# A two-layer encoder trunk on one core: new costs in the planner that writes the instruction order

## The chip, the cores and the metric

The kernel runs on 1 core of one Trainium2 chip. The metric is the device time of one execution in microseconds (us); lower is better. The time of a kernel is the median of its runs.

## The reference, cut to what matters

The input is 2048 frames of 1024 channels in float32, with one conditioning vector c. There are two layers; each computes `x = x + gate * Mixer(RMSNorm(x) * (1 + scale) + shift)`, where shift, scale and gate are linear functions of SiLU(c). A last RMSNorm follows.

```python
# layer 0, RG-LRU
proj = h @ in_w                      # 1024 -> 2 * 1024
xb = causal_dwconv(xb, conv_w) + conv_b            # width 4
gates = sigmoid(einsum('bsni,knij->kbsnj', xg, gate_w) + gate_b)   # 8 blocks of 128, two gates
a_t = exp(-8 * r_t * softplus(-lam));  b_t = sqrt(1 - a_t**2) * i_t * xf
h_t = a_t * h_(t-1) + b_t;  out = (h * silu(zg)) @ out_w
# layer 1, gated DeltaNet, 8 heads of 128, chunks of 64
q, k, v = silu(causal_dwconv(h @ in_w))            # q and k normalised
t_mat = inverse of the unit lower triangle of each chunk
v_new = u_c - w_c @ state;  o_c = q_c @ state + attn_c @ v_new      # chunk after chunk
state = state * e_c + k_c.T @ v_new
out = (rmsnorm(o) * silu(z)) @ out_w
```

## The kernel before

**Work and stages.** Everything large is a product on TensorE (PE). Operands are split into a high and a low part (hi, lo), and each product is hi*hi + hi*lo + lo*hi: 24 matmuls of 128x512 for one panel of 128 output channels and one half of 512 tokens (`products`, matmul on L653). These "panel products" are called mm in the profile (mmo for the output projections). There are 6168 of them. Tokens come in two units of 1024 (u = 0, 1), each with two halves (i = 0, 1). The stages follow one another: conditioning and norm, `in1` of unit 0 and 1 (layer 0), `out1`, `in2` of unit 0 and 1 (layer 1), `out2`. All the rest of a layer is done beside its panel products, on the engines that are free, and with small matmuls that stand between the panel products on PE.

**Layer 0 beside `in1`.** For every block n of 128 channels and every half i: the product of panel x is copied to `xe` (ACT, L713); the convolution is a first tap on GpSimd (POOL, `xf`, L727) and three taps on VectorE (DVE, `xf`, `taps`, L701); `gates_thread` casts the result to `xh` (ACT, L751), subtracts to `xl` (DVE, L754), and multiplies both with the gate weights, three matmuls for each of two gates (PE, `pg`, L760, PSUM buffers of the tag "c", two of them). ACT makes tanh (L810), tanh and exp (L770, L772) and a square root (L783), DVE a scan (L791), POOL the last product `tz` (L798), which goes to memory. The square root is in another table of ACT than the rest, so ACT loads a table before it and after it (ACT_TABLE_LOAD). The panel's hi part is a cast on ACT (`whi`, L639), the lo part a subtraction on POOL (`wlo`, 128x1024, L642). The other conditioning rows are sums on DVE (`acc`, L415).

**Layer 1 beside `in2`.** For every head h: the convolutions as above (taps again L701), products of keys (PE, `pk` L1073, `pkk` L1108, `pqk` L1193), inverses of the 32 x 32 triangles on DVE in 31 pairs of steps (`ttmp` L1228, `tblk` L1231), the larger blocks on PE (`px`, `pr`, "levels"), and then the recurrence, 16 chunks of 128 tokens, of which each is a chain through three engines (`recurrence_thread`): `pp` = k.state, q.state on PE (L1348, L1349), `zt` on DVE (L1357), `py` on PE (L1365), `yt` on ACT (L1371), `pS` on PE (L1377, L1378), `state` on DVE (L1390), and again. Reciprocal square roots of norms are a power on POOL, of 128x4 elements (L249).

**What sets the order.** Nothing is written by hand in order. A planner, class `Weave`, runs when the kernel is built. Each piece of work is a thread (a Python generator) that, before it emits an instruction, yields the engine, an estimated duration in us, and optionally the latency until the thread's next step can start. `Weave.run` always takes the thread whose step can start earliest by these estimates and lets it emit its instruction:

```python
return max(th.t, self.free.get(w[0], 0.0))        # start of a step: thread and engine free
...
self.free[w[0]] = t + w[1]
th.t = t + w[1] + (w[2] if len(w) > 2 else self.LAG[w[0]])
```

On the chip every engine then takes its instructions in that order, one after the other, and waits by semaphores for what they need; an instruction that waits holds up all that stands behind it on its engine. The estimates are in no instruction. They decide only which instruction stands before which, on each of the five queues (PE, ACT, DVE, POOL, and SP, which issues the DMAs). The panel products have the lowest priority and fill what is free on PE.

Of the kernel before, what the change touches and what calls it, by code (L numbers as in the profile page):

```python
# [36 lines left out]
class Event:  # L37
    t = None
# [3 lines left out]
class Slots:  # L42
    """The buffers of a tag, taken in turn."""
# [5 lines left out]
class Hold:  # L49
    """A buffer with several last readers."""  # L50
# [15 lines left out]
class Weave:  # L66
    """Emits threads of instructions in the order of their estimated start.

    Before each step a thread yields the engine, its duration and optionally the latency
    until the next step may start; for a transfer "sp", its bytes and whether to wait for  # L70
    its end. It yields an Event to wait for it, and Slots to take a buffer of them.
    """

    SEEN = 0.92
    LAG = {"pe": 0.2, "act": 0.3, "dve": 0.3, "pool": 0.2}

    def __init__(self):
        self.free = dict.fromkeys(("pe", "act", "dve", "pool", "sp", "dma"), 0.0)
        self.threads = []
        self.now = 0.0  # L80
# [19 lines left out]
    def start(self, th):  # L100
# [8 lines left out]
        return max(th.t, self.free.get(w[0], 0.0))  # L109

    def run(self):
        while self.threads:
# [17 lines left out]
            elif w[0] == "none":  # L130
                th.t = t + max(w[1], 0.0)
            else:
                self.free[w[0]] = t + w[1]
                th.t = t + w[1] + (w[2] if len(w) > 2 else self.LAG[w[0]])
# [4 lines left out]
def trunk_kernel(ctx, tc, x, c, ada_w, ada_b, ada_c, norm_c, final_g, w1, cw1, cb1, gate_w, gate_b, lam, ow1,  # L139
# [24 lines left out]
    # constants  # L164
# [37 lines left out]
    # tags: pool and number of buffers  # L202
# [11 lines left out]
    # free after the queries, before the recurrence ends  # L214
# [29 lines left out]
    STT, EV, CP, TR, MM, M4 = 0.665, 0.605, 0.48, 0.109, 0.2163, 0.218  # L244
# [6 lines left out]
    def softplus(out, src, e, d):  # L251
        # max(x, 0) + log1p(exp(-|x|)), log1p(e) = 2 atanh(e / (2 + e))
# [16 lines left out]
    def finish_columns(layer, part, d, src):  # L269
        # bias, and for the scale (1 + scale) * norm_g  # L270
# [9 lines left out]
    def columns_of(acc, pt):  # L280
        # sums over the partitions, four columns of 128 channels
# [5 lines left out]
    def first_loads_thread():  # L287
        # scale and shift of the first layer, in the order in which they are needed
# [35 lines left out]
    def first_pe_thread():  # L324
        # scale, by the tensor engine
        c_bc, ttok = yield ev("cbc")
        for n in (0, 2):
# [8 lines left out]
            yield "dve", 0.61, 0.13  # L336
# [4 lines left out]
            yield "dve", 0.61, 0.13  # L341
# [6 lines left out]
    def first_dve_thread():  # L348
        # shift, by DVE and the ones
# [47 lines left out]
    def row_halves_thread(parts):  # L397
        # halves of the other conditioning rows, summed over the channels of c by DVE and the ones
        row = tile_([P, D], "g1", "gate0")
        yield ev("gw", 0, 2)  # L400
        for layer, part, d in parts:
# [35 lines left out]
            yield "dve", 0.61  # L437
# [34 lines left out]
    def norm_thread(key, layer, src, t0, slot, before, after, xtags=("b4",) * TB, htag="hf"):  # L472
        # before: what the loads wait for; after: what the writes wait for
# [1248 lines left out]
```

## Time and profile before

| what | value |
|---|---|
| median of 3 runs | 2044.7 us (2042.34 to 2049.82) |
| profiled execution, first to last instruction (span) | 2033.7 us |
| PE busy | 1881.4 us (93%), 10408 matmul records |
| PE weight loads busy | 1526.0 us (75%) |
| DVE busy | 1578.4 us (78%) |
| ACT busy | 1019.8 us (50%) |
| POOL busy | 945.0 us (46%) |
| granted TensorE clock, mean | 0.978 |
| DMA | 263.99 MB, 130 GB/s |

The page gives the span of the profiled execution and no other time of it; the median of the runs is 11.0 us above that span, for what lies before the first and after the last instruction. The busy time of an engine counts from an instruction's start to its end, with what it loses in between: an instruction of DVE that is held up after its start counts as busy. A fp32 matmul of 128x128 is two records. Lines (L653) are lines of the kernel before; the changed kernel's lines are 15 higher below the planner.

### The profile page before, as it was taken

To read this page: it belongs to the slowest core of one execution; us is meant where nothing else is said; L and a number is where in the kernel's file an instruction comes from. 1 tells how busy PE (TensorE), PEld (TensorE's weight loads), DVE (VectorE), ACT (ScalarE), POOL (GpSimd) and SP (SyncE) were. 2 spreads that over 40 slices of the span, in tenths; PEclk is the share of its full clock that TensorE was granted. 3 is DMA by queue.
4 is the path that set the end of the run, shared out by engine and by line. 5 is a ranking of instruction groups with operands and counts; after the bars stand their busy time and mean duration, and the time that the engine had idled before them with its cause. 6 is when DMAs were issued, how large, how long until landed. Compare 5 with 4: busy or idle time off the path is not lost.

```text
span 2033.7 us, 31640 instructions
## 1 busy us (share of the span) xinstructions
PE 1881.4 (93%) x10408; PEld 1526.0 (75%) x10408; DVE 1578.4 (78%) x3176; ACT 1019.8 (50%) x2449; POOL 945.0 (46%) x1487
## 2 busy tenths in 40 slices
PE   6989889888999999999999999998999999999998
PEld 3777667676787777777787787777878777778887
DVE  6788998987744556988887988778888879887654
ACT  3656566454611224456565555554655555655311
POOL 4565665645400137545454653474455546531101
PEclk9999989989999999999999999999999999999999
DMA  8254524333368813436663436343334333466761
GB/s 315 60 150 128 186 98 134 122 109 119 125 195 215 252 54 96 102 70 148 143 144 82 89 86 173 84 113 93 69 91 104 90 79 83 111 184 210 227 197 63
DMA packets 493132, 263.99 MB, mean 130 GB/s; under 512 B 369188, under 2 KB 437028, under 8 KB 492968
## 3 DMA queue, kind: packets, MB, share of 16 engines
q1 hardware_dynamic: 492968, 261.97, 46.7%
q8 instruction: 82, 1.34, 0.3%
q14 instruction: 82, 0.67, 0.1%
HBM read 186.38 MB, written 75.50 MB: 129 GB/s over the span
## 4 chain that ended last, share of the span: by engine, by line
PE 39%; DVE 27%; DMA 8%; POOL 7%; issue 7%; ACT 6%; SPq 3%; DVEq 0%; POOLq 0%; ACTq 0%
PE mm L653 16%; PE mmo L653 12%; DVE xf L701 7%; DVE tblk L1231 3%; DVE ttmp L1228 3%; PE pg L760 2%; DMA raw<-in_w 2%; POOL wlo L642 1%; DVE ec L1100 1%; DMA xt_d<-xb 1%; SPq L515 1%; DVE acc L415 1%; POOL tz L798 1%; POOL xf L727 1%; DMA xt<-x_d 1%
## 5 line engine op out<-in xcount | busy, mean ns | idle before, releaser
L701 DVE SCALAR_TENSOR_TENSOR xf<-xe,cw_s,xf 128x512 f32<-128x512 f32 x384 | 359.8, 940 | 47.7 <-POOL xf L727 24.6
L642 POOL TENSOR_TENSOR wlo<-raw,whi 128x1024 fp32r<-128x1024 f32 x96 | 243.5, 2537 | 134.9 <-ACT whi L639 119.1
L1231 DVE TENSOR_TENSOR tblk<-tblk,ttmp 128x60 f32<-128x60 f32 (+24 forms) x496 | 144.3, 291 | 10.9 <-POOL tblk L1222 0.5
L1228 DVE TENSOR_TENSOR ttmp<-blk,tblk 128x60 f32<-128x60 f32 (+24 forms) x496 | 123.0, 248 | 16.9 <-DMA blk<-blk_d 6.5
L639 ACT CAST whi<-raw 128x1024 fp32r<-128x1024 f32 x96 | 100.2, 1044 | 47.3 <-DMA raw<-in_w 42.9
L716 POOL COPY carry<-xe 128x4 f32<-128x4 f32 x128 | 41.3, 322 | 170.6 <-ACT xe L713 158.8
L713 ACT COPY xe<-mm 128x512 f32<-128x512 f32 x128 | 74.1, 579 | 83.8 <-PE mm L653 79.8
L653 PE MATMUL mmo<-oh,yh 128*128 128x512 f32 x256 | 100.9, 394 | 5.1 <-DVE xr L908 4.7
L653 PE MATMUL mm<-hl_('in2', 1)_12407,whi 128*128 128x512 f32 x256 | 104.8, 410 | 0.0
L653 PE MATMUL mm<-hh_('in2', 0)_5394,whi 128*128 128x512 f32 x256 | 104.7, 409 | 0.0
L653 PE MATMUL mm<-hh_('in2', 0)_5171,whi 128*128 128x512 f32 x256 | 104.3, 407 | 0.3 <-ACT xe L713 0.3
L653 PE MATMUL mm<-hl_('in2', 0)_5395,whi 128*128 128x512 f32 x256 | 104.2, 407 | 0.0
L653 PE MATMUL mm<-hl_('in2', 1)_12235,whi 128*128 128x512 f32 x256 | 104.2, 407 | 0.0
L653 PE MATMUL mm<-hh_('in2', 0)_5394,wlo 128*128 128x512 f32 x256 | 104.1, 407 | 0.0
L653 PE MATMUL mm<-hh_('in2', 1)_12406,whi 128*128 128x512 f32 x256 | 104.0, 406 | 0.0
L653 PE MATMUL mm<-hl_('in2', 0)_5172,whi 128*128 128x512 f32 x256 | 103.8, 406 | 0.0
L653 PE MATMUL mm<-hh_('in2', 0)_5171,wlo 128*128 128x512 f32 x256 | 103.8, 405 | 0.0
L653 PE MATMUL mm<-hh_('in2', 1)_12234,whi 128*128 128x512 f32 x256 | 103.4, 404 | 0.2 <-DVE tz L972 0.2
L653 PE MATMUL mm<-hh_('in2', 1)_12406,wlo 128*128 128x512 f32 x256 | 103.6, 405 | 0.0
L653 PE MATMUL mm<-hh_('in2', 1)_12234,wlo 128*128 128x512 f32 x256 | 103.5, 404 | 0.0
L653 PE MATMUL mmo<-ol,oh 128*128 128x512 f32 (+1 forms) x264 | 102.1, 387 | 0.0
L653 PE MATMUL mmo<-oh,yl 128*128 128x512 f32 x256 | 100.8, 394 | 1.4 <-DVE yl L882 1.4
(326 smaller groups left out, 5910.8 us busy)
## 6 DMA issues: line engine op xcount, KB each, us to landing
raw<-in_w SPq DMA_DIRECT2D x96, 512.0 KB, 4.0
araw<-in_ada_w SPq DMA_DIRECT2D x32, 512.0 KB, 3.7
xt<-x_d SPq DMA_DIRECT2D x32, 512.0 KB, 4.5
xt_d<-xb SPq DMA_DIRECT2D x192, 64.0 KB, 2.4
xk<-xt_d SPq DMA_DIRECT2D x24, 512.0 KB, 4.7
xt<-in_x SPq DMA_DIRECT2D x16, 512.0 KB, 5.3
ada<-in_ada_w SPq DMA_DIRECT2D x16, 512.0 KB, 8.9
y_d<-tz SPq DMA_DIRECT2D x32, 256.0 KB, 2.7
```

The lines of the kernel that those rows point to most:

```text
L415: dve.scalar_tensor_tensor(acc, raw[:, k, :], ck, acc, ALU.mult, ALU.add)
L515: sp.dma_start(out=dst[c_], in_=tb[32 * c_:32 * c_ + 32])
L639: act.copy(hi, raw)
L642: pool.tensor_tensor(lo, raw, f(hi), ALU.subtract)
L653: pe.matmul(pt, lhsT=lhs[a][:, k, :], rhs=rhs[b][:, k, :], start=(k == 0 and n == 0), stop=(k == KT - 1 and n == 2))
L701: dve.scalar_tensor_tensor(xf, xe[:, 1 + j:1 + j + TC], wc[:, j:j + 1], xf, ALU.mult, ALU.add)
L713: act.copy(xe[:, 4:4 + TC], pt)
L716: pool.tensor_copy(out=carry, in_=xe[:, TC:TC + 4])
L727: pool.tensor_scalar(xf, xe[:, 1:1 + TC], cw1_s[:, n, 0:1], cb1_s[:, n:n + 1], ALU.mult, ALU.add)
L760: pe.matmul(pg, lhsT=a[:, g, :], rhs=b, start=(q == 0), stop=(q == 2))
L1228: dve.tensor_tensor(tmp, blk[:, j, j + 1:32].unsqueeze(2).to_broadcast([P, r, c_]), t[:, j, 0:c_].unsqueeze(1).to_broadcast([P, r, c_]), A ...
L1231: dve.tensor_tensor(t[:, j + 1:32, 0:c_], t[:, j + 1:32, 0:c_], tmp, ALU.subtract)
```

## The change

Only what the planner believes is changed. No instruction is added, removed or changed in size: PE has 8577 matmuls in both, POOL and SP 1487 instructions each in both. The one exception is ACT's table loads, which follow from the order: 49 before, 39 now.

```diff
     SEEN = 0.92
-    LAG = {"pe": 0.2, "act": 0.3, "dve": 0.3, "pool": 0.2}
+    LAG = {"pe": 0.21, "act": 0.15, "dve": 0.13, "pool": 0.1}
+    SWITCH = 0.085
+
+    ENGINE = {"dvp": "dve", "mm": "pe"}
...
-        return max(th.t, self.free.get(w[0], 0.0))
+        t = max(th.t, self.free.get(self.ENGINE.get(w[0], w[0]), 0.0))
+        return max(t, self.free["port"]) if w[0] in ("dve", "pool") else t
...
-                self.free[w[0]] = t + w[1]
-                th.t = t + w[1] + (w[2] if len(w) > 2 else self.LAG[w[0]])
+                dur = w[1]
+                if w[0] in ("pe", "mm"):
+
+                    if w[0] == "mm" and self.small:
+                        dur += self.SWITCH
+                    self.small = w[0] == "pe"
+                e = self.ENGINE.get(w[0], w[0])
+                self.free[e] = t + dur
+                if w[0] in ("dve", "pool"):
+                    self.free["port"] = t + dur
+                th.t = t + dur + (w[2] if len(w) > 2 else self.LAG[e])
...
-    STT, EV, CP, TR, MM, M4 = 0.665, 0.605, 0.48, 0.109, 0.2163, 0.218
+    STT, EV, CP, TR, MM, M4 = 0.665, 0.605, 0.48, 0.109, 0.227, 0.221
...
-                yield "pe", dur, 0.0
+                yield "mm", dur, 0.0
                 pe.matmul(pt, lhsT=lhs[a][:, k, :], rhs=rhs[b][:, k, :], start=(k == 0 and n == 0),
...
-                    yield "dve", 0.27
+                    yield "dvp", 0.27
                     zt = tile_([P, P], "zt", "zt")
...
-        yield "pe", 0.38
+        yield "pe", 1.1
         px = ps.tile([P, NTC, TB, 32], F32, tag="c", name="px")
```

So there are four new beliefs. A step of DVE and a step of POOL can't run at the same time ("port"), except steps of DVE that are marked "dvp": those with an input in PSUM, and the transposes and copies between blocks. The latency from one step to the next is about half of what it was for ACT, DVE and POOL. A panel product that follows a small matmul takes 0.085 longer ("mm" after "pe"). Panel products take 0.227 in place of 0.2163, and the levels' groups of small matmuls up to three times as long (the other three are 0.88 to 1.1, 0.4 to 1.0 and 0.9 to 1.1). The rest of the diff marks more steps "dvp" in the same way and removes comments.

The first place is PE in layer 0, unit 1, channel block 3: the gate products (`pg`) of half 0 and half 1. Before, from the last but one product of half 0 to the first of half 1:

```order
1297 L760 MATMUL pg<-xl,gh 128x512
1298 L760 MATMUL pg<-xh,gl 128x512
1299 L653 MATMUL mm<-hl_('in1', 1)_2246,whi 128x512
1300 L653 MATMUL mm<-hh_('in1', 1)_2245,wlo 128x512
1301 L653 MATMUL mm<-hh_('in1', 1)_2245,whi 128x512
1302 L653 MATMUL mm<-hl_('in1', 1)_2246,whi 128x512
1303 L653 MATMUL mm<-hh_('in1', 1)_2245,wlo 128x512
1304 L653 MATMUL mm<-hh_('in1', 1)_2245,whi 128x512
1305 L653 MATMUL mm<-hl_('in1', 1)_2246,whi 128x512
1306 L283 MATMUL adapt<-ones,acc 128x1 x4
1307 L653 MATMUL mm<-hh_('in1', 1)_2245,wlo 128x512
1308 L760 MATMUL pg<-xh,gh 128x512
```

Now, at the same place:

```order
1321 L775 MATMUL pg<-xh,gl 128x512
1322 L775 MATMUL pg<-xh,gh 128x512
1323 L775 MATMUL pg<-xl,gh 128x512
1324 L775 MATMUL pg<-xh,gl 128x512
1325 L668 MATMUL mm<-hh_('in1', 1)_2271,wlo 128x512
1326 L668 MATMUL mm<-hh_('in1', 1)_2271,whi 128x512
1327 L775 MATMUL pg<-xh,gh 128x512
1328 L775 MATMUL pg<-xl,gh 128x512
1329 L775 MATMUL pg<-xh,gl 128x512
1330 L775 MATMUL pg<-xh,gh 128x512
1331 L775 MATMUL pg<-xl,gh 128x512
1332 L775 MATMUL pg<-xh,gl 128x512
```

The gate products have moved later against the panel products, and those of the two halves stand almost together. Counted in panel products between the end of x's own product and the first `pg`: in this block 48 (half 0) and 33 (half 1) before, 80 and 58 now; over the 32 pairs of block and half 32 to 59 before but for the first, 29 to 97 now, and on average some 21 more.

The second place is ACT in layer 0, unit 1, at the square roots (L783, now L798). Before:

```order
318 L783 ACT_TABLE_LOAD
319 L783 ACTIVATE tg<-tg 128x512
320 L736 ACT_TABLE_LOAD
321 L736 ACTIVATE tz<-mm 128x512
322 L783 ACT_TABLE_LOAD
323 L783 ACTIVATE tg<-tg 128x512
```

Now:

```order
302 L798 ACT_TABLE_LOAD
303 L798 ACTIVATE tg<-tg 128x512
304 L728 COPY xe_3736<-mm 128x512
305 L654 CAST whi<-raw_3731 128x1024
306 L798 ACTIVATE tg<-tg 128x512
307 L751 ACT_TABLE_LOAD
```

A tanh that stood between the two square roots has moved behind both, and two of the four table loads of such a pair are gone.

The third place is PE in layer 1, unit 1, one chunk of the recurrence of one head (`state_115`). Before:

```order
5941 L1348 MATMUL pp<-state_115,kt 128x128
5942 L1349 MATMUL pp<-state_115,qt 128x128
5943 L653 MATMUL mm<-hh_('in2', 1)_12234,whi 128x512
5944 L653 MATMUL mm<-hl_('in2', 1)_12235,whi 128x512
5945 L653 MATMUL mm<-hh_('in2', 1)_12234,wlo 128x512
5946 L653 MATMUL mm<-hh_('in2', 1)_12234,whi 128x512
5947 L1365 MATMUL py<-zt,ac 128x128
5948 L653 MATMUL mm<-hl_('in2', 1)_12235,whi 128x512
5949 L653 MATMUL mm<-hh_('in2', 1)_12234,wlo 128x512
5950 L653 MATMUL mm<-hh_('in2', 1)_12234,whi 128x512
5951 L653 MATMUL mm<-hl_('in2', 1)_12235,whi 128x512
5952 L1377 MATMUL pS<-yt,kd 128x128
```

Now:

```order
6024 L1363 MATMUL pp<-state_115,kt 128x128
6025 L1364 MATMUL pp<-state_115,qt 128x128
6026 L668 MATMUL mm<-hh_('in2', 1)_12356,wlo 128x512
6027 L668 MATMUL mm<-hh_('in2', 1)_11958,whi 128x512
6028 L668 MATMUL mm<-hl_('in2', 1)_11959,whi 128x512
6029 L1380 MATMUL py<-zt,ac 128x128
6030 L668 MATMUL mm<-hh_('in2', 1)_11958,wlo 128x512
6031 L668 MATMUL mm<-hh_('in2', 1)_11958,whi 128x512
6032 L1392 MATMUL pS<-yt,kd 128x128
```

Fewer panel products stand between the steps of a chunk. Over the 120 chunks with a state there were on average 4.3 panel products between `pp` and `py` and are 3.2 now, between `py` and `pS` 3.9 and 2.2 now, and between `pS` and the next `pp` (median) 4 and 3 now. The levels and the recurrence of a head as a whole begin later against the panel products, by about 72 (levels) and 56 (recurrence) on average. Over the kernel, the stretches of panel products without a small matmul between them number 593 before and 570 now.

59 lines of the change are left out of this document (30 added, 29 removed).

## The prediction

> **What bounds the kernel now.** I read the page's first two parts, then the stretches by stage, PE's waits in them, and the timeline at one such wait.
>
> ```profile
> span 2033.7 us, 31640 instructions
> PE 1881.4 (93%) x10408; PEld 1526.0 (75%) x10408; DVE 1578.4 (78%) x3176; ACT 1019.8 (50%) x2449; POOL 945.0 (46%) x1487
> PE 39%; DVE 27%; DMA 8%; POOL 7%; issue 7%; ACT 6%; SPq 3%; DVEq 0%; POOLq 0%; ACTq 0%
> ```
>
> PE is busy 93%, but the chain that ended last (third line) runs through PE for 39% only and through DVE and POOL for 34%: PE is the engine with most work, and is held up by the other two. The stretches of layer 0 (`in1`) and layer 1 (`in2`): length, then busy time of PE, weight loads, DVE, ACT, POOL, then the granted clock:
>
> ```profile
> 74.00:555.00 481.00, 429.97 (x1752) 340.49 (x1750) 406.67 (x446) 284.25 (x384) 285.33 (x257) 0.94 0.42 129
> ...
> 725.00:1836.00 1111.00, 1045.98 (x6773) 860.47 (x6772) 916.43 (x2351) 607.70 (x1830) 588.73 (x1102) 0.99 0.43 104
> ```
>
> Layer 0 (first row) leaves PE idle 481.0 - 430.0 = 51.0 us and at a clock of 0.94; layer 1 (second) 1111.0 - 1046.0 = 65.0 us at 0.99. In both, the busy times of DVE and POOL add up to more than the stretch (692 of 481, 1505 of 1111). What they do to PE, in layer 0 at 467 us:
>
> ```profile
> 466.89 0.50 PE L760 MATMUL pg<-xh,gh 128*128 128x512 f32 x1 [0.42 <-ACT xh L751]
> 467.86 2.34 POOL L642 TENSOR_TENSOR wlo<-raw,whi 128x1024 fp32r<-128x1024 f32 x1 [0.45 <-ACT whi L639]
> 467.87 2.88 DVE L701 SCALAR_TENSOR_TENSOR xf<-xe,cw_s,xf 128x512 f32<-128x512 f32 x1
> 470.68 0.68 DVE L754 TENSOR_TENSOR xl<-xf,xh 128x512 fp32r<-128x512 f32 x1
> 471.41 0.53 PE L760 MATMUL pg<-xl,gh 128*128 128x512 f32 x1 [4.02 <-DVE xl L754]
> ```
>
> A tap of DVE that starts 0.01 us after POOL's wlo ends 0.55 us after it and takes 2.88 us; PE has reached the gate product and waits 4.02 us for the xl behind that tap. The old planner let the two run side by side. What a tap takes alone and in the mean, and what wlo takes (min/median/max in the view of one line):
>
> ```profile
> L701 DVE SCALAR_TENSOR_TENSOR xf<-xe,cw_s,xf x384: 700/749/2921, 59.1 to 1795.2; 128x512 f32<-128x512 f32 x192
> L701 DVE SCALAR_TENSOR_TENSOR xf<-xe,cw_s,xf 128x512 f32<-128x512 f32 x384 | 359.8, 940 | 47.7 <-POOL xf L727 24.6 <-POOL xf L944 17.5 <-POOL xe L707 2.2
> ```
>
> The mean, 940 ns, is 191 over the median: 384 taps lose some 73 us after their start. The same stall costs twice, as the granted clock shows (stretch, PE busy, clock):
>
> ```profile
> 466.00:471.00 5.00, 0.97 (x4) 1.00 0.45 157
> 471.00:475.00 4.00, 3.59 (x9) 0.59 0.00 0
> ```
>
> In the 5 us around that stall PE is busy for 0.97 us, and in the 4 us after it the clock is 0.59, half speed most of the time. Over layer 0 that is (1 - 0.94) x 481 = 28.9 us of lost PE time.
>
> **The change, layer 0.** PE's waits in 74 to 555 us:
>
> ```profile
> PE pg L760 <- DVE xl L754: 31.2, 17, 4.5
> ...
> PE pg L760 <- ACT xh L751: 6.1, 8, 1.3
> 105.52 11.60 PE mm L653 x51
> ```
>
> The gate products wait 31.2 + 6.1 = 37.3 us, 4.5 us at most. A panel matmul takes 11.60 / 51 = 0.2275 us (last row, from the chain), so the 21 panel matmuls by which the gate products have moved on average are 4.8 us, more than the longest wait. If xl keeps its time against the panel products, all these waits go, and with them the half clock behind them: 37.3 + 28.9 = 66.2 us is the upper end, zero the lower (the wait moves elsewhere). What is late next is DVE. All 66.2 would leave 415 us for 406.7 us of DVE time. The stretch in which DVE is densest is:
>
> ```profile
> 1000.00:1280.00 280.00, 263.40 (x1736) 216.79 (x1735) 240.27 (x625) 165.08 (x499) 152.09 (x277) 0.99 0.51 118
> 74.00:555.00 481.00, 108.54 (x93) 0.94 0.42 129
> ```
>
> There it is busy 240.27 / 280 = 0.86. The second row is of the taps alone: 93 in layer 0 take 108.5 us, where the median would make 69.7, so 38.9 us are blocking. If half of that goes (the order still sends taps and wlo side by side), DVE needs 406.7 - 19.4 = 387.3 us, at 0.86 that is 450 us. I take 481 - 450 = **31 us** of gain, near the middle of the range.
>
> The gate products of two halves now stand together and need four PSUM buffers out of two, so the third waits until ACT has emptied the first. That is covered, since ACT waits for PE there (below: 33.4 us in 32 waits) and the gate product between and two panel matmuls lie in between; uncovered, it would be one tanh of ACT in each of 16 pairs. Ten table loads of 1.283 us (row below) leave ACT: 12.8 us, on an engine busy 284 of 481, so I cost them at nothing; the idle 197 us cover them, and 12.8 us is the most they could bring.
>
> ```profile
> ACT tg L810 <- PE pg L760: 33.4, 32, 2.8
> L783 ACT ACT_TABLE_LOAD x24 | 30.8, 1283 | 0.4
> SPq L802 <- POOL tz L798: 127.7, 29, 12.7
>   PEld mm L653: 1.3, 3
> ```
>
> On SP, the write of y waits 127.7 us for POOL's tz, with loads of panels queued behind it; tz now comes later by those 4.8 us or less. It costs nothing, as PE waits 1.3 us in all for a wlo (last row, of those who wait for L642). Without that slack, 29 such waits times 4.8 us would be 139 us, which nothing in the trace suggests.
>
> **Layer 1.** PE's waits in 725 to 1836 us, and one of them in the timeline:
>
> ```profile
> PE pp L1348 <- DVE state L1390: 16.6, 13, 2.4
> PE py L1365 <- DVE zt L1357: 9.9, 8, 1.6
> PE pk L1073 <- DVE tblk L1231: 9.0, 3, 4.4
> PE pqk L1193 <- DVE qt L961: 5.7, 5, 1.5
> PE pk L1073 <- DVE ttmp L1228: 2.5, 2, 1.7
> PE pp L1348 <- DVE ttmp L1228: 1.5, 1, 1.5
> PE pp L1348 <- DVE tblk L1231: 1.2, 1, 1.2
> ...
> 1053.77 0.49 PE L1348 MATMUL pp<-state,kt 128*128 128x128 f32 x2 [0.78 <-DVE state L1390]
> ...
> 1054.24 0.48 PE L653 MATMUL mm<-hh_('in2', 0)_5171,whi 128*128 128x512 f32 x1
> 1054.56 0.40 PE L653 MATMUL mm<-hl_('in2', 0)_5172,whi 128*128 128x512 f32 x1
> 1054.79 0.39 PE L653 MATMUL mm<-hh_('in2', 0)_5171,wlo 128*128 128x512 f32 x1
> ```
>
> The four waits for the inverses (tblk, ttmp) are 9.0 + 2.5 + 1.5 + 1.2 = 14.2 us: PE stood at a small matmul whose input DVE had queued behind inverse steps which the old plan thought done. The new plan reserves POOL's time and places what follows the inverses about 72 panel matmuls (16 us) later. I take these **14 us** as gained. The waits of the recurrence (16.6 + 9.9 = 26.5) I leave as they are: DVE should be nearer the plan, but the plan leaves it less time (first rival). Upper end: all 65.0 us of idle time and 11 us of clock. Lower end: 103 us lost, worked out below.
>
> The plan reserves too much in one place. A power on POOL and inverse steps on DVE:
>
> ```profile
> 1146.58 1.01 POOL L249 TENSOR_TENSOR rk<-ssk,mhalf 128x4 f32<-128x4 f32 x1
> 1146.59 0.24 DVE L1231 TENSOR_TENSOR tblk<-tblk,ttmp 128x49 f32<-128x49 f32 x1
> 1146.87 0.20 DVE L1228 TENSOR_TENSOR ttmp<-blk,tblk 128x42 f32<-128x42 f32 x1
> ```
>
> Two steps with two inputs begin and end inside 1.01 us of POOL, unblocked, while the plan keeps them out. The Trainium skill (SBUF — State Buffer, Who interferes with whom) has it otherwise: a DVE instruction with two SBUF inputs and a GpSimd instruction that reads SBUF exclude each other for the whole instruction. By that rule the plan would be right about these powers too, the pqk waits (5.7 us) would go as well, and the sum below would be 1992. For the tap and wlo above the trace agrees with it (2.88 us); for the powers it does not, and the measurement decides.
>
> **The rest.** The first panel matmul after a small one comes 0.32 us before the next, the following 0.23 (1054.24, 1054.56, 1054.79): 0.09 us for an exposed weight load. 23 fewer such switches save **2 us**; none or more of them hidden is 0 to 2. The tail does not wait:
>
> ```profile
> 1887.04 139.53 PE mmo L653 x638
> ```
>
> The last state now comes some 28 panel matmuls later (5517 of 6168 in place of 5489), and the blocks that need it begin at 5760, which is (5760 - 5517) x 0.2275 = 55 us of slack; if it were used up, PE would wait by what is over. The start and out1 I leave as they are: the order changes little there.
>
> **Sum.** 31 + 14 + 2 = 47 us. The profiled span of 2033.7 becomes 1986.7. The median of the runs lies 11.0 us above that span, which I carry over: **1998 us**, 2.3% less. About 0.5% is what a measurement of this kernel can tell from no change, that is 2034.5 to 2054.9.
>
> **Rivals.** First, slower: the recurrence runs dry. A chunk has lost 1.1 + 1.7 + 1.0 = 3.8 panel matmuls of cover (from 4.3 to 3.2, 3.9 to 2.2, 4 to 3), 0.86 us. If DVE is as late as before, 120 chunks wait 103 us more. For it:
>
> ```profile
> DVE zt L1357 <- PE pp L1349: 11.2, 21, 1.4
> L1371 ACT ACTIVATE yt<-py x128: 255/277/290, 862.5 to 1885.9; 128x128 f32<-128x128 f32 x128
> ```
>
> Only in 21 of 120 chunks did DVE stand ready for pp, so it came late to most. Against it: yt takes 0.28 us and has 2.2 x 0.2275 = 0.50 us. With two thirds of the 103 us and the 14 gone, it is 2044.7 - 33 + 69 = 2081. It decides from 33 / 120 = 0.28 us lost per chunk on. Chance 0.21.
>
> Second, no change: DVE and POOL set the pace in layer 0. Their common time (692 us of busy time in 481) keeps its length, PE no longer waits at pg but for PSUM buffers that DVE and ACT empty, and only the 2 us remain: 2043. For it speaks DVE's 85% in that stretch, against it the 38.9 us of blocking and the half clock. Chance 0.12.
>
> Third, more of the same: all of layer 0's 66 and half of layer 1's 65 and of its clock, 66 + 33 + 6 + 2 = 107 us: 1938. It needs DVE busy without a gap. Chance 0.15. That the change does nothing is excluded, since the queues differ nearly from the start.
>
> My case has the remaining 0.52; its own range is 1975 to 2030. Faster 0.52 + 0.15 = 0.67, same 0.12, slower 0.21. The range reaches into the first and the third case, 1950 to 2062, and leaves out some 0.08 below and 0.12 above.
>
> **What would show it.** Right: pg waits under 10 us in layer 0, its clock at 0.97 or more, the stretch of in1 near 450 us; pk's waits for tblk gone; ACT 13 us less busy; pp and py waits still near 26 us. Wrong: pp and py waits over 60 us, or layer 0 as long as before with new waits of mm. If taps and wlo collide as often as now (mean still 940 ns) and the time falls all the same, the port itself was not the reason, only the room on PE's queue.

## The result and the profile after

The changed kernel takes **2182.6 us** (median of 4 runs, 2180.33 to 2191.25). The kernel before, on the same chip, takes 2043.5 us. The ratio is 1.068 (interval 1.064 to 1.072): 6.8% slower, where 2.3% faster was predicted. A run takes 1.7 us longer than its own span (2180.96 us and 2179.2 us for the profiled run here). So of the 11.0 us between the median before and its profiled span only some 2 us lie outside of the span; the rest is that the profiled execution was a quick one. The stages below, which are compared with that execution, therefore differ by a few us more than the medians do.

The page of the changed kernel: span, busy times, the chain that ended last, the taps of DVE, and the granted clock in 40 slices:

```profile
span 2179.2 us, 31523 instructions
...
PE 1947.7 (89%) x10408; PEld 1543.3 (71%) x10408; DVE 1498.7 (69%) x3176; ACT 1005.8 (46%) x2439; POOL 907.2 (42%) x1487
...
PEclk9999888999999999999999888999999999989999
...
PE 38%; DVE 17%; DMA 14%; ACT 10%; POOL 7%; issue 6%; SPq 4%; DVEq 0%; POOLq 0%; ACTq 0%
...
L716 DVE SCALAR_TENSOR_TENSOR xf<-xe,cw_s,xf 128x512 f32<-128x512 f32 x384 | 312.9, 819 | 55.2 <-POOL xf L742 38.4
```

The change did what it was written to do. The taps take 819 ns on average in place of 940, DVE is busy for 80 us less and POOL for 38 us less: fewer of their steps collide. Yet the busy share of every engine is smaller in a longer span, and PE is busy 66 us *more* with the same matmuls, at a lower clock. The 117 instructions fewer are the ten table loads and instructions that only wait for semaphores. DMA has 14% of the chain in place of 8%.

To see where the time went, both kernels are cut where a stage's first panel matmul starts. The two units of layer 1 (`in2`) and the tail in the kernel before; columns as in the prediction, length, PE busy, weight loads, DVE, ACT, POOL, clock:

```profile
725.00:1276.00 551.00, 518.36 (x3290) 424.73 (x3288) 455.07 (x1167) 298.86 (x894) 294.83 (x555) 0.99 0.46 108
1276.00:1838.00 562.00, 529.62 (x3493) 437.34 (x3493) 463.30 (x1191) 309.64 (x940) 294.35 (x550) 0.99 0.41 101
1838.00:2033.70 195.70, 188.56 (x982) 157.54 (x980) 113.77 (x151) 58.14 (x136) 22.46 (x57) 0.99 0.55 175
```

The changed kernel: `out1`, the two units of layer 1, the tail, and below them a stretch of layer 0:

```profile
551.00:759.00 208.00, 191.93 (x793) 151.62 (x792) 116.81 (x160) 42.55 (x53) 21.05 (x26) 0.95 0.74 215
759.00:1373.00 614.00, 545.92 (x3274) 436.08 (x3273) 437.88 (x1175) 301.39 (x893) 286.75 (x557) 0.94 0.42 98
1373.00:1970.00 597.00, 548.47 (x3443) 435.30 (x3441) 424.62 (x1152) 306.90 (x915) 285.18 (x545) 0.96 0.40 98
1970.00:2179.20 209.20, 200.21 (x1050) 162.34 (x1048) 123.33 (x196) 66.23 (x170) 23.87 (x62) 0.99 0.52 159
74.00:555.00 481.00, 412.49 (x1667) 324.99 (x1666) 355.01 (x399) 260.55 (x362) 258.02 (x250) 0.93 0.37 108
```

Layer 1 has grown from 551 + 562 = 1113 to 614 + 597 = 1211 us, by 98. Its PE idle time went from 1113 - 518.36 - 529.62 = 65.0 to 1211 - 545.92 - 548.47 = 116.6 us (+51.6), and PE's busy time from 1048.0 to 1094.4 us (+46.4), with the clock at 0.94 and 0.96 in place of 0.99. `out1` went from 189 (536 to 725 us) to 208 us, the tail from 196 to 209, layer 0 from 496 (40 to 536 us) to 511 (40 to 551). Together that is 98 + 19 + 13 + 15 = 145 us, the difference of the two spans (the medians differ by 139 us). The last row is the stretch of layer 0 that the prediction used.

What PE waited for in the kernel before, where the prediction does not show it, and in the changed kernel (total, times, longest, us):

```profile
PE mm L653 <- ACT xe L713: 3.4, 2, 3.1
...
PE pS L1377 <- ACT yt L1371: 2.2, 4, 1.1
...
PE mm L653 <- DVE tz L738: 0.2, 1, 0.2
```

```profile
PE mm L668 <- ACT xe L728: 26.3, 16, 4.0
PE mm L668 <- DVE tz L753: 25.8, 9, 4.7
PE pg L775 <- DVE xl L769: 18.1, 7, 7.9
...
PE pS L1392 <- ACT yt L1386: 11.1, 19, 1.7
PE px L1314 <- ACT tf L1303: 10.4, 5, 4.2
...
PE pqk L1208 <- DVE qt L976: 7.8, 6, 3.2
PE pr L1297 <- ACT tf L1288: 7.8, 2, 7.0
PE pr L1324 <- ACT tf L1316: 7.6, 4, 2.9
...
PE py L1380 <- DVE zt L1372: 5.1, 6, 1.8
...
PE pp L1363 <- DVE state L1405: 3.6, 6, 1.1
```

The waits at `pg` fell from 37.3 to about 19 us, those of the recurrence (`pp`, `py`) from 26.5 to 8.7 us. New waits took their place: panel products that wait for a PSUM buffer (mm for `xe` and for layer 0's `tz`, 52.1 us, 3.6 before), the levels (`px`, `pr`, 25.8 us for ACT, none before) and `pS` for `yt`.

By engine and stage, the sums of these rows say where the time went. In layer 1, PE's waits for DVE fell from 56.9 to 44.1 us, and its waits for ACT rose from 3.0 to 65.6 us (`xe` 26.0, `px` and `pr` 25.8, `yt` 10.3); all of them together went from 63.9 to 115.1 us, which is nearly all of PE's idle time there. In layer 0 they went from 54.4 to 72.1 us, and 25.8 us of that are the waits for `tz`; only 0.3 us are for `xe`.

The waits for `tz` have one origin. Its tile has two SBUF buffers, and a buffer comes free when the write of y to memory (`y_d<-tz`) has landed. ACT's tanh (L751), or the table load just before it, waits for that write (ACT's wait in the changed kernel; before it was 2.5 us in all):

```profile
ACT L751 <- DMA y_d<-tz: 66.6, 10, 8.5
```

One such place, in layer 0 of the changed kernel:

```profile
420.64 1.29 POOL L813 TENSOR_TENSOR tz<-tz,tg 128x512 f32<-128x512 f32 x1
421.95 6.01 SPq L817 DMA_DIRECT2D y_d<-tz  x2
424.45 1.28 ACT L751 ACT_TABLE_LOAD   x1 [6.54 <-DMA y_d<-tz]
425.75 0.60 ACT L751 ACTIVATE tz<-mm 128x512 f32<-128x512 f32 x1
426.38 0.69 DVE L753 SCALAR_TENSOR_TENSOR tz<-tz,mm 128x512 f32<-128x512 f32 x1 [0.31 <-ACT tz L751]
...
427.12 0.78 PE L668 MATMUL mm<-hh_('in1', 1)_2271,whi 128*128 128x512 f32 x1 [4.67 <-DVE tz L753]
```

The gate products stand later, so POOL's last product is late, the write of y is late, ACT stands 6.54 us for the buffer, DVE's product, which frees the panel's PSUM buffer, comes after that, and PE waits 4.67 us. The row of waits for `tz` counts nine; in the eight over 0.5 us ACT had just waited for such a write, in seven of them for 4.9 to 8.5 us.

In layer 1 the wait has also turned round. DVE's wait for the last product of a chunk, before:

```profile
DVE state L1390 <- PE pS L1378: 29.5, 31, 2.8
```

and in the changed kernel:

```profile
DVE state L1405 <- PE pS L1393: 69.6, 55, 3.3
```

DVE now stands ready 55 times in place of 31, while PE is behind. One such place, in layer 1, in the timeline of the changed kernel:

```profile
1240.00 0.38 SPq L1193 DMA_DIRECT2D vn<-v_d  x1
...
1242.92 1.28 ACT L1197 ACTIVATE vn<-vn,nk 128x128 f32<-128x128 f32 x4 [2.54 <-DMA vn<-v_d]
...
1244.10 0.56 ACT L728 COPY xe<-mm 128x512 f32<-128x512 f32 x1
...
1244.72 0.79 PE L668 MATMUL mm<-hh_('in2', 0)_5362,whi 128*128 128x512 f32 x1 [4.04 <-ACT xe L728]
```

The copy `xe`, which would free PSUM for PE, stands in ACT's queue behind `vn`, and `vn` waits for a load that SP issued only at 1240.00. PE waits 4.04 us. Over the kernel, ACT's waits for transfers grew from 183 to 394 us (for `vn` alone from 7.3 to 48.0). The clock around that place (columns as before: the stretch and its length, then PE busy, and the clock after POOL):

```profile
1236.00:1240.00 4.00, 4.00 (x21) 3.38 (x20) 3.32 (x14) 1.31 (x3) 1.14 (x5) 1.00 0.93 210
1240.00:1244.70 4.70, 0.68 (x7) 0.49 (x5) 4.29 (x5) 2.13 (x6) 3.75 (x3) 0.81 0.36 80
1244.70:1246.00 1.30, 1.28 (x3) 1.09 (x4) 1.23 (x3) 0.00 (x0) 1.21 (x2) 0.50 0.33 50
1246.00:1250.00 4.00, 4.00 (x11) 3.09 (x11) 3.96 (x6) 2.69 (x7) 2.25 (x5) 0.53 0.24 36
1250.00:1252.00 2.00, 2.00 (x11) 1.60 (x10) 0.12 (x1) 0.23 (x1) 1.84 (x7) 1.00 0.23 35
```

PE runs at half speed for some 5 us after the stall (1.30 us at 0.50 and 4.00 us at 0.53), which loses 0.65 + 1.88 = 2.5 us on top of the 4. Over the whole kernel, (1 - clock) times time is 45 us before and 115 us now, 70 us more, and PE's busy time grew by 66 us; PE's idle time grew from 152 to 232 us. That is 66 + 79 = 145 us, the growth of the span. So the question is why the order makes PE stop more often.

### The profile page after: what moved, and what is told of

Its sections match the earlier page's. It is cut to its first block, busy times and chain, and to the rows that moved or that the text cites. A ratio compares the mean times of both kernels' runs of the same rounds, so it can differ in the third digit from the quotient of the medians.

```text
span 2179.2 us, 31523 instructions
## 1 busy us (share of the span) xinstructions
PE 1947.7 (89%) x10408; PEld 1543.3 (71%) x10408; DVE 1498.7 (69%) x3176; ACT 1005.8 (46%) x2439; POOL 907.2 (42%) x1487
## 4 chain that ended last, share of the span: by engine, by line
PE 38%; DVE 17%; DMA 14%; ACT 10%; POOL 7%; issue 6%; SPq 4%; DVEq 0%; POOLq 0%; ACTq 0%
PE mm L668 18%; PE mmo L668 10%; DVE xf L716 4%; DMA raw<-in_w 3%; POOL wlo L657 2%; DMA pq<-q_d 2%; DVE ttmp L1243 1%; PE pS L1392 1%; PE pg L775 1%; DVE tblk L1246 1%; DMA y_d<-tz 1%; ACT junk L1099 1%; SPq L1181 1%; PE py L1380 1%; DVE ec L1115 1%
## 5 line engine op out<-in xcount | busy, mean ns | idle before, releaser
L668 PE MATMUL mm<-hh_('in2', 0)_5362,whi 128*128 128x512 f32 x256 | 107.5, 420 | 13.4 <-ACT xe L728 12.7
L668 PE MATMUL mm<-hh_('in2', 1)_12356,whi 128*128 128x512 f32 x256 | 107.2, 419 | 9.6 <-ACT xe L728 8.6
L668 PE MATMUL mm<-hh_('in2', 1)_11958,whi 128*128 128x512 f32 x256 | 105.7, 413 | 5.1 <-ACT xe L728 4.1
L668 PE MATMUL mm<-hh_('in2', 0)_5319,whi 128*128 128x512 f32 x256 | 105.5, 412 | 2.8 <-DVE tz L987 2.0
L668 PE MATMUL mm<-hl_('in2', 0)_5363,whi 128*128 128x512 f32 x256 | 107.1, 418 | 0.0
L668 PE MATMUL mm<-hh_('in2', 1)_11958,wlo 128*128 128x512 f32 x256 | 106.4, 416 | 0.0
L668 PE MATMUL mm<-hl_('in2', 1)_12357,whi 128*128 128x512 f32 x256 | 106.0, 414 | 0.0
L668 PE MATMUL mm<-hh_('in2', 0)_5362,wlo 128*128 128x512 f32 x256 | 105.8, 413 | 0.0
L668 PE MATMUL mm<-hh_('in2', 1)_12356,wlo 128*128 128x512 f32 x256 | 105.7, 413 | 0.0
L668 PE MATMUL mm<-hl_('in2', 1)_11959,whi 128*128 128x512 f32 x256 | 105.0, 410 | 0.0
```

Of the source, the lines that this page charges most:

```text
L668: pe.matmul(pt, lhsT=lhs[a][:, k, :], rhs=rhs[b][:, k, :], start=(k == 0 and n == 0), stop=(k == KT - 1 and n == 2))
```

## The experiments

Every ratio is against the kernel before, with its 95% interval. "Levels at" is the mean position of the levels, counted in panel products from the start: 4025 before, 4096 in the changed kernel. A letter in an expectation stands for the theory that its own text describes. The runs "on the kernel before" are the changed kernel with all its new costs put back to the old numbers (SWITCH 0.0) and the port not asked for (`return t`); their edits are shown against that form.

### Which part of the change costs

The first theory was that one of the parts does it. Port alone on the kernel before:

```diff
-        return t
+        return max(t, self.free["port"]) if w[0] in ("dve", "pool") else t
```

> The kernel before with one new belief alone: steps of DVE and POOL exclude each other (with the exemptions). In its order the gate products stand 64.8 panel products after x's product on average (before 44.2, changed kernel 65.5), table loads 47. Theory A (the shared port is what makes the changed order slow: the plan now has DVE and POOL later than the chip, PE and ACT are ordered to that late plan, and DVE starves): slower by most of the 139 us, 2130 to 2190, DVE busy share near 70%, clock near 0.95. Theory B (the shorter latencies cost the time, because they took away the cover of ACT and DVE): 1990 to 2050. Theory C (the old numbers were a good draw, and any other order loses some per cent): slower by 2 to 5%, like the other two parts alone.

The latencies alone:

```diff
-    LAG = {"pe": 0.2, "act": 0.3, "dve": 0.3, "pool": 0.2}
+    LAG = {"pe": 0.21, "act": 0.15, "dve": 0.13, "pool": 0.1}
```

> The kernel before with the new latencies alone (0.21, 0.15, 0.13, 0.1 in place of 0.2, 0.3, 0.3, 0.2). Gate products at 42.0 panel products, table loads 55, chunk steps of the recurrence 3.0 and 2.9 panel products apart (before 4.0 and 3.7). Theory A: within 1% of 2043, since no port is in it. Theory B: slower by most of the 139 us, 2130 to 2190, with waits for ACT (yt, xe, tf) as in the changed kernel. Theory C: slower by 2 to 5%.

TensorE's costs alone (0.2163 to 0.227 and its like, the levels' groups, SWITCH 0.085):

```diff
-    SWITCH = 0.0
+    SWITCH = 0.085
...
-    STT, EV, CP, TR, MM, M4 = 0.665, 0.605, 0.48, 0.109, 0.2163, 0.218
+    STT, EV, CP, TR, MM, M4 = 0.665, 0.605, 0.48, 0.109, 0.227, 0.221
```

> The kernel before with the new TensorE costs alone (panel matmul 0.227, 0.085 more after a small one, the levels' groups about 1.1). Gate products at 39.5 panel products, table loads 61. Theory A and B: within 1% of 2043, the durations of TensorE being nearer the trace. Theory C: slower by 2 to 5%.

The changed kernel without the port (the first diff undone):

> The changed kernel without the shared port, latencies and TensorE costs new. Gate products at 40.4, table loads 61. Theory A: the time comes back, 2010 to 2060. Theory B: it stays near 2180. Theory C: anywhere from 2080 to 2160.

| kernel | us | ratio | interval |
|---|---|---|---|
| port alone | 2191.9 | 1.074 | 1.064 to 1.084 |
| latencies alone | 2088.0 | 1.023 | 1.013 to 1.033 |
| TensorE costs alone | 2141.3 | 1.049 | 1.039 to 1.059 |
| changed, no port | 2191.7 | 1.074 | 1.063 to 1.085 |

Every part alone slows the kernel, and they don't add: the port costs 7.4% and the other two together 7.4%, all three 6.8%. So theory A, by which the port is the cause, falls: the port alone does cost as much as the whole change, but without it the time does not come back. Theory B has the run without the port right (it stays near 2180) and falls with the latencies alone, and theory C's 2 to 5% fits two of the parts but neither the port nor the run without it. The parts also do different things. In layer 1 PE waits 60.8 us for DVE and 49.8 us for ACT with the port alone, and 100.2 us for DVE and 10.0 us for ACT in the changed kernel without the port (before: 56.9 and 3.0).

The new costs of TensorE are close to measured ones: in the trace of before, a panel matmul starts 0.227 us after another (median, at full clock), the first after a small one keeps the next back by 0.314 us, and the first group of the levels takes 1.09 us.

### Is any new order worse?

The rival was that the order of before is a lucky one, and any shift of the estimates loses it. Two nudges of the last digit, which reorder the queues but change nothing in substance:

```diff
-    LAG = {"pe": 0.2, "act": 0.3, "dve": 0.3, "pool": 0.2}
+    LAG = {"pe": 0.2, "act": 0.3, "dve": 0.301, "pool": 0.2}
```

> The kernel before with DVE's latency 0.301 in place of 0.3, a number without any physical meaning; some 430 of 15000 rows of TensorE's and 550 of DVE's order read otherwise. Theory C (the old numbers are a good draw, every other order loses): 2060 to 2150. Theory D (the time follows how late the small work stands against the panel products, and only a shift of that distance costs): gate products at 43.1 panel products (before 44.2), levels and recurrence within 2 panel products of before, so 2030 to 2060.

```diff
-    STT, EV, CP, TR, MM, M4 = 0.665, 0.605, 0.48, 0.109, 0.2163, 0.218
+    STT, EV, CP, TR, MM, M4 = 0.665, 0.605, 0.48, 0.109, 0.2164, 0.218
```

> The kernel before with a panel matmul of 0.2164 in place of 0.2163. Some 1055 rows of TensorE's order read otherwise, gate products at 45.6 panel products, table loads 53. Theory C: 2060 to 2150. Theory D: 2030 to 2060.

They took 2054.1 us, ratio 1.005 (1.003 to 1.008), and 2058.5 us, 1.008 (1.006 to 1.011). Theory D holds for these two, C does not. These small reshuffles cost 0.5 to 0.8%, some tenth of the loss. They touch 430 and 1055 of some 15000 rows of PE's order, though, while the change moves nearly all; a reshuffle of that size that means nothing was not run, so how much of the loss any order so different would have is open.

### Layer 0 alone, and the sums that moved

The port shared only until layer 0's projections are planned, with the old latencies and costs:

```diff
+        return max(t, self.free["port"]) if self.shared and w[0] in ("dve", "pool") else t
...
+                w.shared = False
```

> The kernel before with the shared port alone, and that only up to the end of the projections of layer 0; from the output projection on the planner is the old one. In the run with the port alone, the projections of layer 0 took 18 us less than before (238 and 240 us in place of 246 and 250), and the later stages lost 172. Theory E (the port as the planner has it is right for layer 0 and wrong for layer 1): 2015 to 2035, the projections of layer 0 at 478 us. Theory C: 2060 to 2150, the later stages losing again in an order that is not the old one.

It took 2062.1 us, ratio 1.009 (1.005 to 1.012), above theory E's range. Layer 0 was 478 us in place of 496, as hoped, but `out1` 213 in place of 189, 14.7 us of which are one wait at its end. The first row is of the DVE sums of the conditioning rows in this kernel (line, count, min/median/max in ns, first and last start), the second PE's wait at the start of layer 1:

```profile
L431 DVE SCALAR_TENSOR_TENSOR acc<-araw,c_col,acc x56: 707/750/2876, 138.2 to 685.1; 128x512 f32<-128x512 f32 x56
```

```profile
PE mm L669 <- DVE hh_('in2', 0)_5414 L589: 14.7, 1, 14.7
```

The same rows of the kernel before and of the changed one:

```profile
L415 DVE SCALAR_TENSOR_TENSOR acc<-araw,c_col,acc x56: 704/746/2890, 131.5 to 516.1; 128x512 f32<-128x512 f32 x56
```

```profile
L430 DVE SCALAR_TENSOR_TENSOR acc<-araw,c_col,acc x56: 710/750/2944, 132.6 to 690.4; 128x512 f32<-128x512 f32 x56
```

Before, the last sum starts at 516 us, in layer 0. With the port it starts at 685 or 690 us, in `out1`: the sums have a low priority and now find DVE or the port taken. Of the loads that feed them (512 KB each), 14 of 32 are issued after `out1` has begun in the changed kernel and 18 with the port in layer 0, none in the kernel before. Of the stages shown, `out1` has most traffic (DMA share 0.74, 215 GB/s in its row above). To test that, the sums alone are taken out of the port:

```diff
-                    yield "dve", STT, 0.13
+                    yield "dvp", STT, 0.13
```

In the changed kernel:

> The changed kernel with one more exemption: the DVE steps of the conditioning sums don't reserve the port. In the changed kernel 14 of the 32 loads for these sums and 28 of their 64 DVE steps ran after the output projection of layer 0 had begun (before: none); in this order none do. Theory F (the spilled sums and their 512 KB loads are what lengthens out1): out1 back from 209 to 186 to 195 us, layer 1 as in the changed kernel (1200 to 1220), time 2150 to 2170. If out1 stays near 209, something else in it is late.

2148.1 us, ratio 1.052 (1.048 to 1.055), just under the expected range. `out1` came back to 190 us as expected, and layer 0 took 493 us in place of 511. With the same line in the kernel with the port in layer 0:

> The run with the port in layer 0 alone and old latencies and costs, with the conditioning sums exempt. Levels at 4025, as before. Theory F and D together: the projections of layer 0 478 to 485 us (the 17 us of gain stay, less what the sums take back), out1 near 189, layer 1 near 1113: 2020 to 2040, faster than before. If layer 0 goes back to 496, the gain there had only been the sums pushed out of it, and the time is near 2045.

2037.8 us, ratio 0.998 (0.996 to 1.000): the kernel before. `out1` is 187 us, but layer 0 is 498 us again (in an execution of 2050 us, 12 above the median, so a part of these may not be its own). So most of the 18 us that layer 0 had gained were the sums it had put off, and the port in layer 0 brings nothing measurable in all. This is the version nearest to a gain, and it is none.

### POOL's small steps

The prediction had seen that the plan reserves the port for powers on POOL that don't block DVE. Their work is small (128x4), their time is not (groups by line of the kernel before: busy us, mean ns of one, idle before):

```profile
L249 POOL TENSOR_TENSOR rk<-ssk,mhalf 128x4 f32<-128x4 f32 x32 | 35.9, 1121 | 2.7
L249 POOL TENSOR_TENSOR ro<-so,mhalf 128x4 f32<-128x4 f32 x32 | 35.2, 1100 | 2.7
L249 POOL TENSOR_TENSOR rq<-ssq,mhalf 128x4 f32<-128x4 f32 x32 | 34.0, 1061 | 2.7
```

That is 105.1 us during which no DVE step with SBUF inputs may be planned. In the trace of before DVE's steps run on all the same: 80 `tblk` steps start inside a power (78 of them in one of 128x4) and overlap no other step of POOL; they have a median of 218 ns, and 221 that overlap no POOL step have 214. 13 taps start so and have 745 ns, as do those alone; 29 that start inside a copy of four columns have 751. The changed kernel with these and other small POOL steps (12 places: powers, memsets, carries) out of the port:

```diff
-    ENGINE = {"dvp": "dve", "mm": "pe"}
+    ENGINE = {"dvp": "dve", "mm": "pe", "plp": "pool"}
...
-        yield "pool", 1.5
+        yield "plp", 1.5
```

> The changed kernel with POOL's small steps (powers of 128x4, copies of four columns) no longer reserving the port; wlo, tz, xf, eh, el still do. Gate products at 58.8 panel products, levels 46 panel products earlier than in the changed kernel. Theory A' (the plan is too slow because it keeps DVE out of the port for powers that do not block it): the layer-1 stages come back to within 20 us of before, time 2060 to 2110. Theory C: 2130 to 2200.

**2102.8 us**, ratio 1.029 (1.026 to 1.032): 80 us less than the changed kernel and within the expected range, though layer 1, at 1155 us, is still 42 us above before and not within 20. This is the largest single piece. The opposite, on the kernel before, shares the port between these small steps and DVE only:

```diff
-        return t
+        return max(t, self.free["port"]) if w[0] in ("dve", "plp") else t
...
-                if w[0] in ("dve", "pool"):
+                if w[0] in ("dve", "plp"):
```

> The kernel before, and of the change only this: POOL's small steps (powers, memsets, carries) and DVE's steps from SBUF keep each other out in the plan; wlo, squares and norms of POOL share nothing. Theory A (these reservations are by themselves what costs the changed kernel its 80 us): 2043 plus 50 to 90, that is 2095 to 2135. Theory B (they cost only on top of the rest of the change, since the plan of before leaves DVE's queue with slack): within 1% of before, 2030 to 2065.

2102.1 us, ratio 1.028 (1.024 to 1.031): the false reservations cost 57 us by themselves. Theory A holds, B falls. Some of PE's waits in that kernel:

```profile
PE pg L775 <- DVE xl L769: 35.8, 18, 5.4
...
PE mm L668 <- ACT xe L728: 16.0, 5, 5.7
...
PE px L1285 <- DVE tf L1278: 6.9, 6, 4.3
```

PE waits for `xe` (3.4 us before) and at the levels (`px`), as in the changed kernel, and at `pg` as long as before; its levels stand at 4075. The Trainium skill (SBUF — State Buffer, Who interferes with whom) has a DVE instruction with two SBUF inputs and a GpSimd instruction that reads SBUF exclude each other. For the large steps the traces agree (taps beside `wlo`, 2.88 us); for the powers they do not (218 ns against 214), and a plan that follows the rule there loses 57 to 80 us.

### Both repairs, and what is left

The changed kernel with both the small steps and the sums out of the port:

> The changed kernel with both repairs: POOL's small steps and the conditioning sums don't reserve the port. Levels stand at 4050 panel products on average as with the first repair alone (before 4025, changed kernel 4096). Theory F: out1 186 to 195 in place of 206, time 2075 to 2095. Theory D (layer 1 goes by the place of the levels): layer 1 near 1155 again, so still above before in all.

2096.2 us, ratio 1.026 (1.023 to 1.029), 1 us above theory F's range; layer 1 is near 1155 as theory D had it. Some 54 us stay, and by the profiles most of them are in layer 1 (578 + 582 = 1160 us against 1113, by the cuts above). Are they from the new costs? The repaired port with each pair of old and new latencies and TensorE costs:

> The kernel with both repairs, and TensorE's old costs (panel matmul 0.2163, no switch, short levels), so that panel products run ahead in the plan and small work stands later: levels at 4131 (before 4025, with both repairs 4050, port alone 4131). Theory D: layer 1 as with the port alone, 1220 to 1245, and a time of 2140 to 2170. If more cover is what the accurate costs lack, layer 1 gets shorter than with both repairs and the time is 2030 to 2070.

> The changed kernel with both repairs and the old latencies, the third corner of the square of latencies and costs. If the new latencies alone are what is left: 2040 to 2060. If the TensorE costs alone: 2090 to 2105. If the shared port: 2085 to 2125, with no order among the four corners by latency or cost.

> The kernel before, with the shared port in which POOL's small steps and the sums are exempt, and nothing else of the change. Theory G (the 54 us that are left with both repairs come from the new latencies and TensorE costs): within 1% of before, 2025 to 2065. Theory H (they come from the shared port itself, which puts steps of DVE and POOL one behind the other that would have done better overlapped): 2 to 4% slower, 2085 to 2125.

| with the repaired port | us | ratio | interval |
|---|---|---|---|
| old latencies, old TensorE costs | 2088.5 | 1.021 | 1.017 to 1.025 |
| old latencies, new TensorE costs | 2077.0 | 1.015 | 1.011 to 1.019 |
| new latencies, old TensorE costs | 2116.9 | 1.037 | 1.033 to 1.040 |
| new latencies, new TensorE costs | 2096.2 | 1.026 | 1.023 to 1.029 |

The repaired port alone costs 2.1% (43 us): theory H, and most of what is left. With the old latencies alone put back it was 2077.0 us, which none of that run's three expectations had. The new latencies add 1.1 to 1.6 points, and the new TensorE costs take 0.6 to 1.0 back. Without any port the same TensorE costs had cost 4.9%, so what a part does depends on the others. A layer 1 of 1220 us and more for the old TensorE costs, as one theory had it, did not come: it was 1169.

What can a port that reserves only for real collisions lose? It puts the levels later: at panel product 4130 in the kernel with the repaired port alone. That was tested by itself, on the kernel before:

```diff
         tt_d = yield ev("tt", u, h)
+        yield "none", 16.0
```

> The kernel before, with the inverses' levels held back by 16 us in the plan: they stand at panel product 4130 on average in place of 4025, as in the kernels with a shared port, and everything else keeps its costs. Theory E (late levels, and the recurrence behind them, are what the order with a shared port loses in layer 1): 2 to 4% slower, 2085 to 2125. Theory F (the place of the levels does not matter, only what stands too early does): within 1%, 2025 to 2065.

**2129.9 us**, ratio 1.039 (1.036 to 1.043), a little above the upper end of theory E; F falls. Layer 0 and `out1` are as before (499 and 189 us), layer 1 is 577 + 606 and the tail 217. In its trace DVE stands and waits for PE more often:

```profile
DVE state L1406 <- PE pS L1394: 84.8, 58, 4.2
...
DVE zt L1373 <- PE pp L1365: 37.0, 53, 1.3
```

against 29.5 us (31 times) and 11.2 us (21 times) before. PE in turn waits 85.6 us for DVE and 17.2 us for ACT in layer 1 (before 56.9 and 3.0). In the tail it waits 3.3 us only; the tail is longer because more of the recurrence's small matmuls have moved into it (1174 matmul records in place of 982). So a later place of the levels costs time in this order. The place alone does not set the time, though: four kernels have the levels at 4130 or 4131 and take 2088.5 (repaired port alone), 2116.9 (with the new latencies), 2129.9 (this one) and 2191.9 us (port alone). This one has the repaired port's place without the port and loses twice as much, so the place does not explain what the repaired port loses.

## Why the prediction was wrong

**The sign of layer 1.** "I take these 14 us as gained" is the step that failed worst. It took the later place of the levels (by 72 panel products) as room for DVE and priced only what comes off PE's waits for DVE. These did fall, by 12.8 us (56.9 to 44.1): the waits at `pk` and `pp` for the inverses from 14.2 to 4.6 us (4.9 us of new ones stand at `pqk`), and those of `pp` and `py` in the recurrence by 17.8. What the new order makes PE wait for elsewhere was put at nothing, and it is 62.6 us more for ACT (3.0 to 65.6), with a clock of 0.94 and 0.96 in place of 0.99 behind it. So PE is idle 51.6 us more and busy 46.4 us longer, and layer 1 is 98 us longer. A late start also has a price of its own: the levels held back alone, by 105 panel products, cost 85 us.

**"The plan reserves too much in one place"** was right, and priced only as 5.7 us that are not gained. It is 57 us alone and 80 us within the change. The mistake was to price the reservations by a wait that the trace of before shows. A reservation is no wait: it moves the steps behind it in the plan, and with them the order of the other queues, and the price is in what stops there.

**Layer 0, 31 us.** The waits at `pg` were halved, not removed (37.3 to 19.3 us), and the stage was 15 us longer with a clock of 0.93, no better than before. The step that failed is the one on the write of y: "tz now comes later by those 4.8 us or less. It costs nothing, as PE waits 1.3 us in all for a wlo". It looked at the loads that stand behind that write on SP, and not at the SBUF buffer that the write holds. ACT waits 68.7 us for that buffer (2.5 before), and PE 25.8 us for `tz` (0.2 before). No run takes that wait away, with a third buffer for example, so what it costs in all is not shown. "What is late next is DVE" was the wrong engine: DVE had 0.74 of its time busy (355.0 of 481). The port alone did shorten the stage, to 478 us, and the 18 us were mostly the sums that it put off; with the sums held in their stage, the port gained nothing that could be measured.

**"The start and out1 I leave as they are: the order changes little there."** It changed: the sums moved from layer 0 into `out1`, 19 us there. The comparison of the two orders had this in it, and I did not follow low-priority work past the end of its stage.

**The tail.** "The tail does not wait" was right: PE waits 1.8 us there. (By the traces the recurrence's last product stands behind 5530 panel products before and 5549 now, not 28 apart, which leaves some 48 us of slack.) It grew by 13 us all the same, because later work falls into it (1050 matmul records in place of 982, PE busy 200.2 us in place of 188.6).

**What held.** ACT is busy 14.0 us less (12.8 expected from ten table loads), which changes nothing; the taps collide less. The 11.0 us that the sum carries over as time outside of the span are for the most part a quick execution, as said above; that is well within the range. The first rival had the sign but not the mechanism: it decides where `pp` and `py` wait more, and they wait 17.8 us less; only `pS` waits more for `yt` (11.1 us, 2.6 before). The second had the time wrong, but it is the one that named PE's wait for PSUM buffers that DVE and ACT empty. The third falls. The half clock was rightly read as a second price for each stall, but only as something to be won.

**What stays open.** Why the order makes ACT late in layer 1 is seen at single places, not isolated. Nor is why the truer TensorE costs lose 4.9% without a port and win with one, while the latencies lose in both. In the kernel with the TensorE costs alone the levels come earlier (3985), and it loses too, so place alone does not explain it. A plausible reading, argued and not shown: the old numbers erred in both directions, and the panel time that was too short and the latencies that were too long kept slack in front of DVE steps that the plan thinks faster than they are.

## What to carry to other kernels

A planner's number that is truer by itself need not give a better order: here each part of the change lost alone, so each correction is measured alone and together. A mutual exclusion is planned at most for the forms whose trace shows it (here large steps beside large steps), since a false reservation moves all that stands behind it; even the repaired one cost 2.1% here. And when an order moves, price the chain that now starts later, the low-priority work that slips into the next stage and the buffers that a late write still holds, on every engine, not only the waits that it removes.

## What the runs showed of the hardware

- A wait of PE costs twice, and short ones suffice: half-speed stretches come in steps of some 3.4 us (3.4, 6.8, 10.2, 13.7). In the trace of before, 8 of 11 idle gaps of 2 to 3 us were followed by one within 3.5 us, in the changed kernel 12 of 17; of gaps of 4 us and more, all 4 and all 9. There are 20 such stretches before and 38 after. The Trainium skill (TensorE: Matmul & The Clock Gate, Part 1) puts the drop to half rate after an idle window of about 3.4 us; the step agrees, while gaps of 2 to 3 us already lead to it here.
- Where a gap lies matters. In each of the two traces all half-speed stretches start on one grid of 3.413 us. After a full-speed step of that grid in which PE was idle for 2.0 us or more, the next step was at half speed in 41 of 41 cases (both traces); after 1 to 2 us in 16 of 83, after less than 1 us in 1 of 1001. All 8 gaps of 2 to 3 us that were not followed by half speed lie across a grid line, with less than 2 us on either side.
- Powers on POOL of 128x4 take about 1.1 us and do not slow a DVE step with two SBUF inputs (218 ns against 214).
